# Keys of a sparse-attention layer projected transposed and rotated by a partition shuffle

## Chip, core and metric

The kernel runs on one core of a Trainium2 chip. The metric is the device time of one execution in microseconds (us). A profiled execution gives the rows quoted below; its engines are PE (TensorE matmuls), PEld (TensorE weight loads), DVE (VectorE), ACT (ScalarE), POOL (GpSimd) and SP (SyncE, which issues the DMAs).

## What is computed

Two layers over 256 tokens of width 1024. Each normalises its input, projects it once, and gives one part of the projection to a recurrent mixer (HGRN2) and one to a sparse attention with 8 query heads and 2 key/value groups of 128 dimensions. The part that matters here:

```python
q = partial_rope(q, pos)
ks = partial_rope(ks, pos)
kw = partial_rope(kw, pos)
k_cmp = compress(kc, *cmp_k)
v_cmp = compress(vc, *cmp_v).astype(jnp.float32)
k_cmp = partial_rope(k_cmp, cmp_end).astype(jnp.float32)
```

`ks`, `kw` are the keys of the selected-block and the window branch, `k_cmp` the 15 compressed keys. `partial_rope` rotates the first 32 of 128 dimensions only: with x1 the first 16 and x2 the next 16, it gives x1·cos − x2·sin and x2·cos + x1·sin; the other 96 pass through.

## The kernel before

**Precision and weights.** Every float32 matmul operand is split in a high and a low part, and a product takes three matmuls (high·high, high·low, low·high). Weights stream through a ring of units: a DMA lands in `raw`, ACT copies it to `whi` (L202) and DVE subtracts to `wlo` (L203). Eight converted units and five raw ones are held; a unit's place comes free with its last matmul. `Hhi` and `Hlo` are the transposed, normalised input with its dimensions on the partitions.

**The order of the work** is written out by hand. One layer runs: query projection (`a_pair`), forget gates, compressed keys and values (`kcvc`), `kv_w` (window keys and values), `compress` 0, `kv_s` (selected keys and values), `compress` 1, and then the attention, spread between the projections that follow. Later steps are handed to `later`, which emits them once a count of matmul time has passed (`tick`); `flush` emits them at once. Each engine then executes its own instructions in the order emitted.

**Keys, values and compress before.** `kv_s` multiplies with the tokens of one tile (`a`, 128 tokens) on the output partitions and 512 columns (256 of keys, 256 of values); `kv_w` does 256 key columns and 280 value and gate columns apart (L368 to L370, `mm_a`). So keys come out with tokens on the partitions: `rope` (L384) rotates them, ACT copying 96 dimensions (L386) and DVE doing four small operations (L390 to L393). Eight units of matmul time later `turn_k` turns them with PE transposes (L552), and `split_k` (L539) splits the result into `kTh` (copied by ACT, L540) and `kTl` (subtracted by DVE, L541), with the dimensions on the partitions as the scores (L608 to L610) want them. The compressed keys take the same way: `second` projects them (L519), `rope` rotates them, `third` transposes them (L531). Values go through `vals` (L558): a copy `vhi` on ACT (L560), then a subtraction `vlo` on DVE (L561). In `kv_w` a sigmoid on ACT (L587) reads the gate columns of the same bank after that.

**PSUM banks.** There are three banks of tag `mm`, two of `s`, two of `t`, one of `o`. In `kv_w` the values of tile 0 take one `s` bank, those of tile 1 the other, and `compress` 0 (L490 to L493, output `ps_s`) the first again: its first matmul waits for the last reader of tile 0's values, which is the sigmoid of L587. Two engines that read one bank do so one after the other.

Of the kernel before, what the change touches and what calls it, by code (L numbers as in the profile page):

```python
# [10 lines left out]
F32 = mybir.dt.float32  # L11
# [8 lines left out]
T = 256  # L20
# [11 lines left out]
C_KC, C_KS, C_KW, C_NG, C_NZ = 5120, 5632, 6144, 6656, 6680  # L32
SCALE = HD ** -0.5
LEVELS = (1, 2, 4, 8, 16, 32)
CTW = 544
SAFE = 1e-35
UW = 1072
RING = 8
# [3 lines left out]
CP = (2.0, 3.0)  # L42
L1 = (3.0, 3.0)
L2 = (5.0, 5.0)
L3 = 3.0
LQ = 4.0
LK = 8.0
LH = 10.0
PW = 7.0
PS = 48.0  # L50
# [2 lines left out]
def shape_tables():  # L53
    def rope(pos, scale):
        inv = np.float32(500000.0) ** (np.float32(-2.0) * np.arange(RH, dtype=np.float32) / np.float32(32))
        ang = pos.astype(np.float32)[:, None] * inv.astype(np.float32)[None, :]
        c = np.cos(ang.astype(np.float64)).astype(np.float32)
        s = np.sin(ang.astype(np.float64)).astype(np.float32)
        return np.concatenate([c, c, -s, s], axis=1) * np.float32(scale)

    t = np.arange(T)
    j = np.arange(128)
    parts = [np.eye(128, dtype=np.float32)]
    for scale in (SCALE, 1.0):
        r = rope(t, scale)
        parts.append(r[:128])
        parts.append(r[128:])
    e = 16 * np.arange(NCMP) + 31
    rc = np.zeros((128, 64), np.float32)
    rc[:NCMP] = rope(e, 1.0)  # L70
    parts.append(rc)
    for a in range(NT):
        cm = np.where(e[None, :] <= (a * 128 + j)[:, None], 0.0, NEG)
        parts.append(np.concatenate([cm, np.full((128, 1), NEG / 10)], axis=1).astype(np.float32))
    sel = np.zeros((128, 2, 30), np.float32)
    for part in range(2):
        for a in range(2):
            for g in range(G):
                for n in range(NCMP):
                    sel[34 * part + 16 * g + n + a, a, 15 * g + n] = 1.0  # L80
            sel[34 * part + 32 + a, a, :] = 1.0
    parts.append(sel.reshape(128, 60))
    f = np.concatenate(parts, axis=1).astype(np.float32)
# [9 lines left out]
    return f, f2, m  # L93


def build(ctx, tc, A, out):
# [150 lines left out]
    rope_k = [ct[:, 256 + 64 * a:320 + 64 * a] for a in range(NT)]  # L247
    rope_c = ct[:, 384:448]
    cmask = [ct[:, 448 + 16 * a:464 + 16 * a] for a in range(NT)]
    sel = ct[:, 480:540].rearrange("p (a n) -> p a n", a=2)  # L250
    cm3 = cp.tile([128, 384], BF, name="cm3")

    posh = cp.tile([128, 128], F32R, name="posh")
# [119 lines left out]
    def mm_b(ps, un, u, c):  # L373
        for i in range(4):
# [112 lines left out]
    def compress(l, i, ring, KC):  # L487
# [25 lines left out]

        def second():
            y2 = tb()
            n = 96 if i else NCMP
            for g in range(G):
                lhs = act3[:, g, :] if i else act[:, g * 15:(g + 1) * 15]
                P.matmul(out=y2[0:n, g * 128:(g + 1) * 128], lhsT=lhs, rhs=w2[:, i, :], start=True, stop=True)  # L519
            y2v = y2[0:n, 0:256].rearrange("p (g d) -> p g d", g=2)  # L520
            if i:
                S.copy(out=vcs[0:96], in_=y2v)
                V.tensor_tensor(out=vcs[32:64], in0=y2v[32:64], in1=vcs[32:64].bitcast(F32), op=OP.subtract)
                return
            kst = sp.tile([128, 2, 128], F32, name="kst", tag="st", bufs=2)
            rope(kst[0:NCMP], y2v, rope_c, 2, 1.0, NCMP)

            def third():
                tp = tb()
                for g in range(G):  # L530
                    P.transpose(out=tp[:, g * 128:g * 128 + NCMP], in_=kst[0:NCMP, g, :],  # L531
                                identity=ident[0:NCMP, 0:NCMP])
                split_k(256, NCMP, tp.rearrange("p (g n) -> p g n", g=4)[:, 0:2, 0:NCMP])

            later(L3, third, "c0")

        later(L1[i], sums, "c%d" % i)

    def split_k(o, n, src):  # L539
        S.copy(out=kTh[:, :, o:o + n], in_=src)  # L540
        V.tensor_tensor(out=kTl[:, :, o:o + n], in0=src, in1=kTh[:, :, o:o + n].bitcast(F32), op=OP.subtract)  # L541

    KOFF = ((128, 0), (272, 400))

    def keys(a, br, ps):
        kst = sp.tile([128, 2, 128], F32, name="kst", tag="st", bufs=2)
        rope(kst, ps.rearrange("p (g d) -> p g d", g=2), rope_k[a], 2, 1.0)

        def turn_k():
            tp = tb()  # L550
            for g in range(G):
                P.transpose(out=tp[:, g * 128:(g + 1) * 128], in_=kst[:, g, :], identity=ident)  # L552
            o = KOFF[br][a]
            split_k(o, 128, tp[:, 0:256].rearrange("p (g t) -> p g t", g=2))

        later(LK, turn_k, "k")

    def vals(a, br, ps):  # L558
        hi, lo = vhi[:, a, br, :], vlo[:, a, br, :]
        S.copy(out=hi, in_=ps)  # L560
        V.tensor_tensor(out=lo, in0=ps, in1=hi.bitcast(F32), op=OP.subtract)  # L561

    def kv_s(ring):
        un = ring.take(4)
        for a in range(NT):
            ps = mmb()
            for u in range(4):
                mm_a(ps, un[u], u, a, 0, 512)
                if a:
                    ring.done(1)  # L570
            keys(a, 0, ps[:, 0:256])
            vals(a, 0, ps[:, 256:512])

    def kv_w(ring):
        un = ring.take(4)
        for a in range(NT):
            ps = mmb()
            for u in range(4):
                mm_a(ps[:, 0:256], un[u], u, a, 0, 256)
            keys(a, 1, ps[:, 0:256])  # L580
            ps = sb_()
            for u in range(4):
                mm_a(ps[:, 0:280], un[u], u, a, 256, 280)
                if a:
                    ring.done(1)
            vals(a, 1, ps[:, 0:256])
            S.activation(out=gt[:, a].rearrange("p h b -> p (h b)"), in_=ps[:, 256:280], func=AF.Sigmoid)  # L587

    def attend(a, g):
# [8 lines left out]
        def scores(i):  # L598
# [16 lines left out]
                mk = [cm3[:, 128:256]] * 2  # L615
                cm = ps[:, 128:144]
            else:
                flush("k")
                qk(ps[:, 0:272], 0, 272)
                p2 = sb_()  # L620
                qk(p2[:, 0:256], 272, 528)
# [553 lines left out]
```

## Time and profile before

| | |
|---|---|
| runs of the kernel before | 559.06 us median (558.58 to 559.13, 3 runs) |
| profiled execution, its own time | 558.97 us |
| its span, first to last instruction | 557.2 us |
| busy: PE / PEld / DVE / ACT | 543.8 / 487.6 / 398.8 / 333.0 us |
| `kv_w` to `compress` 1, first layer | about 72 to 105 us from the span's start |
| the same, second layer | about 340 to 374 us |

The span leaves about 1.8 us around it. A group of the profile is a source line with an engine and an operation; a view by time shows start, duration and, in brackets, the idle time before an instruction and what ended it. Matmul durations overlap, since the next one starts while the last still drains: the distance from one start to the next is what a matmul costs.

### The profile page before, as it was taken

The page shows a single profiled execution, that of the slowest core. Times are in us where ns is not written, and L with a number is a line of the kernel's source. Part 1 is how long each engine was busy: PE and PEld are TensorE (multiplying, and loading weights), DVE is VectorE, ACT ScalarE, POOL GpSimd, SP SyncE. Part 2 cuts the span into 40 slices and gives each one's busy share as a digit, 9 for nine tenths or more (in the row PEclk, how much of TensorE's full clock was granted, in tenths as well). Part 3 has the DMA queues.
Part 4 walks back from the last instruction along what each step waited for, and adds up shares of the span by engine and source line. Part 5 has one row for each costly group of instructions (what it writes and reads, how often), then busy time and mean ns, then how long its engine had stood idle before and what let it go on. Part 6 is the DMA issues. An engine that isn't in the chain of part 4 may idle for free.

```text
span 557.2 us, 9821 instructions
## 1 busy us (share of the span) xinstructions
PE 543.8 (98%) x3675; PEld 487.6 (88%) x3675; DVE 398.8 (72%) x883; ACT 333.0 (60%) x632; POOL 9.6 (2%) x18
## 2 busy tenths in 40 slices
PE   7999999999999999999999999989999999999994
PEld 4889998899888989988888999979988888898884
DVE  4887997889777277563687599888987654866422
ACT  6576537865567685562557763677646768746311
POOL 4000000000000001001000000000000000000000
PEclk9999999999999999999999999999999999999998
DMA  8698548965146158566385755697433622956111
GB/s 302 195 314 257 146 127 266 304 193 152 39 117 190 35 166 291 185 191 188 115 262 162 228 154 152 196 302 256 125 101 84 174 85 63 303 172 200 59 38 44
DMA packets 72197, 96.56 MB, mean 173 GB/s; under 512 B 3383, under 2 KB 49357, under 8 KB 72142
## 3 DMA queue, kind: packets, MB, share of 16 engines
q1 hardware_dynamic: 71854, 95.33, 55.2%
q8 instruction: 31, 0.51, 0.4%
q10 hardware_dynamic: 288, 0.52, 0.2%
q14 instruction: 24, 0.20, 0.1%
HBM read 93.75 MB, written 2.10 MB: 172 GB/s over the span
## 4 chain that ended last, share of the span: by engine, by line
PE 88%; DMA 4%; ACT 3%; DVE 2%; issue 1%; SPq 0%; ACTq 0%; DVEq 0%
PE ps_mm L378 10%; PE ps_mm L380 10%; PE ps_mm L379 10%; PE ps_mm L368 9%; PE ps_mm L369 9%; PE ps_mm L370 9%; PE ps_mm L1005 4%; PE ps_mm L1007 4%; PE ps_mm L1006 4%; DMA raw<-in_w_in 2%; ACT whi L202 2%; PE ps_t L668 2%; DMA raw<-in_cmp_w_v 2%; PE ps_s L608 1%; DVE wlo L203 1%
## 5 line engine op out<-in xcount | busy, mean ns | idle before, releaser
L203 DVE TENSOR_TENSOR wlo<-raw,whi 128x1024 fp32r<-128x1024 f32 (+1 forms) x168 | 203.0, 1223 | 60.7 <-ACT whi L202 56.3
L202 ACT CAST whi<-raw 128x1024 fp32r<-128x1024 f32 (+1 forms) x168 | 174.9, 1052 | 87.9 <-PE ps_mm L379 24.5
L378 PE MATMUL ps_mm<-Hhi,whi 128*128 128x256 f32 x448 | 127.5, 285 | 0.0
L380 PE MATMUL ps_mm<-Hhi,wlo 128*128 128x256 f32 x448 | 125.7, 281 | 0.0
L379 PE MATMUL ps_mm<-Hlo,whi 128*128 128x256 f32 x448 | 125.7, 281 | 0.0
L368 PE MATMUL ps_mm<-whi,Hhi 128*128 128x512 f32 (+1 forms) x256 | 102.0, 399 | 0.7 <-ACT Hhi L355 0.7
L370 PE MATMUL ps_mm<-whi,Hlo 128*128 128x512 f32 (+1 forms) x256 | 98.9, 386 | 0.0
L369 PE MATMUL ps_mm<-wlo,Hhi 128*128 128x512 f32 (+1 forms) x256 | 98.8, 386 | 0.0
L379 PEld LDWEIGHTS ps_mm<-Hlo,whi 128*128 128x128 f32 x448 | 84.5, 189 | 0.1
L378 PEld LDWEIGHTS ps_mm<-Hhi,whi 128*128 128x128 f32 x448 | 84.3, 188 | 0.1
L380 PEld LDWEIGHTS ps_mm<-Hhi,wlo 128*128 128x128 f32 x448 | 84.4, 188 | 0.0
L370 PEld LDWEIGHTS ps_mm<-whi,Hlo 128*128 128x128 f32 x256 | 48.7, 190 | 10.3 <-DVE Hlo L356 0.3
L368 PEld LDWEIGHTS ps_mm<-whi,Hhi 128*128 128x128 f32 x256 | 48.9, 191 | 8.5 <-ACT Hhi L355 1.1
L369 PEld LDWEIGHTS ps_mm<-wlo,Hhi 128*128 128x128 f32 x256 | 49.0, 191 | 7.5 <-DVE wlo L203 0.5
L630 ACT ACTIVATE sB<-ps_s,nm 128x256 f32<-128x256 f32 (+1 forms) x40 | 16.9, 428 | 12.2 <-DVE nm L627 11.5
L627 DVE CUSTOM_DVE_ANT_0 ps_s<-ps_s,cm 128x128 f32<-128x128 f32 (+1 forms) x64 | 22.4, 371 | 1.9 <-PE ps_s L610 0.7
L671 DVE TENSOR_TENSOR sB<-ps_t,sB 128x512 fp32r<-128x512 f32 x12 | 8.3, 688 | 20.1 <-ACT sB L670 20.1
L1005 PE MATMUL ps_mm<-whi,sN 128*128 128x512 f32 x48 | 19.0, 397 | 0.0
L1006 PE MATMUL ps_mm<-wlo,Hhi 128*128 128x512 f32 x48 | 18.9, 395 | 0.0
L1007 PE MATMUL ps_mm<-whi,Hlo 128*128 128x512 f32 x48 | 18.9, 395 | 0.0
L1006 PE MATMUL ps_mm<-wlo,sN 128*128 128x512 f32 x48 | 18.9, 394 | 0.0
L1007 PE MATMUL ps_mm<-whi,sN 128*128 128x512 f32 x48 | 18.9, 394 | 0.0
(299 smaller groups left out, 921.0 us busy)
## 6 DMA issues: line engine op xcount, KB each, us to landing
raw<-in_w_in SPq DMA_DIRECT2D x112, 512.0 KB, 4.5
raw<-in_w_out SPq DMA_DIRECT2D x32, 512.0 KB, 4.3
raw<-in_w_in SPq DMA_DIRECT2D x8, 536.0 KB, 4.1
raw<-in_cmp_w_k SPq DMA_DIRECT2D x16, 256.0 KB, 3.4
raw<-in_cmp_w_v SPq DMA_DIRECT2D x16, 256.0 KB, 3.2
sB<-in_x SPq DMA_DIRECT2D x3, 512.0 KB, 3.6
sB<-in_post_norm SPq DMA_DIRECT2D x2, 512.0 KB, 4.8
xs<-sB SPq DMA_DIRECT2D x4, 256.0 KB, 2.0
```

The source lines that it names most:

```text
L202: S.copy(out=hi, in_=raw)
L203: V.tensor_tensor(out=lo, in0=raw, in1=hi.bitcast(F32), op=OP.subtract)
L368: P.matmul(out=ps, lhsT=hh, rhs=wh, start=k == 0, stop=False)
L369: P.matmul(out=ps, lhsT=hh, rhs=wl, start=False, stop=False)
L370: P.matmul(out=ps, lhsT=hl, rhs=wh, start=False, stop=k == KT - 1)
L378: P.matmul(out=ps, lhsT=wh, rhs=hh, start=k == 0, stop=False)
L379: P.matmul(out=ps, lhsT=wh, rhs=hl, start=False, stop=False)
L380: P.matmul(out=ps, lhsT=wl, rhs=hh, start=False, stop=k == KT - 1)
L627: V.tensor_tensor_reduce(out=sb[b], in0=sb[b], in1=mk[b], scale=-1.0, scalar=3e38, op0=OP.add, op1=OP.min, accum_out=nm[:, i, b:b + 1])
L1005: P.matmul(out=ps, lhsT=hi, rhs=wh, start=first, stop=False)
L1006: P.matmul(out=ps, lhsT=hi, rhs=wl, start=False, stop=False)
L1007: P.matmul(out=ps, lhsT=lo, rhs=wh, start=False, stop=last)
```

## The change

Keys are projected with the weights as the stationary operand and all 256 tokens as the moving one (L551 to L553 of the changed kernel, in `keys`), one group after the other, into one bank: 48 matmuls of 256 columns for each branch. The dimensions are on the partitions at once, so `turn_k`, `third` and their transposes go. `rope_t` rotates in place: a shuffle of the 32 partitions swaps the halves into `sh`, and three DVE operations multiply with tables and add, on 32 partitions. `split_k` then reads the bank directly. `second` projects the compressed keys in one matmul with 30 columns. Values of both token tiles in `kv_s` share one bank and are split by one ACT and one DVE operation. The table `ct` shrinks from 544 to 352 columns of 128 partitions; a table `kt` of 32 partitions and 544 columns is loaded later, in `consts2`.

```diff
-CTW = 544
+CTW = 352
+KTW = 544
...
+        nc.sync.dma_start(out=kt, in_=A["kt"])
...
+    def rope_t(x, tab, n):
+
+        c, s = (t[:, None, :].to_broadcast([32, G, n]) for t in tab)
+        sh = sp.tile([128, 512], F32, name="sh", tag="st", bufs=2)[0:32, 0:G * n].rearrange("p (g n) -> p g n", g=G)
+        V.stream_shuffle(out=sh, in_=x[0:32], mask=SWAP)
+        V.tensor_tensor(out=sh, in0=sh, in1=s, op=OP.mult)
+        V.tensor_tensor(out=x[0:32], in0=x[0:32], in1=c, op=OP.mult)
+        V.tensor_tensor(out=x[0:32], in0=x[0:32], in1=sh, op=OP.add)
...
+            if not i:
+                P.matmul(out=y2[:, 0:G * NCMP], lhsT=w2[:, 0, :], rhs=act, start=True, stop=True)
+                y2v = y2[:, 0:G * NCMP].rearrange("p (g n) -> p g n", g=G)
+                rope_t(y2v, rope_c, NCMP)
+                split_k(kTh[:, :, 256:256 + NCMP], kTl[:, :, 256:256 + NCMP], y2v)
+                return
...
-    def keys(a, br, ps):
-        kst = sp.tile([128, 2, 128], F32, name="kst", tag="st", bufs=2)
-        rope(kst, ps.rearrange("p (g d) -> p g d", g=2), rope_k[a], 2, 1.0)
-
-        def turn_k():
-            tp = tb()
-            for g in range(G):
-                P.transpose(out=tp[:, g * 128:(g + 1) * 128], in_=kst[:, g, :], identity=ident)
-            o = KOFF[br][a]
-            split_k(o, 128, tp[:, 0:256].rearrange("p (g t) -> p g t", g=2))
-
-        later(LK, turn_k, "k")
...
+    def keys(un, br):
+        ps = mmb()
+        for g in range(G):
+            out = ps[:, g * T:(g + 1) * T]
+            for k in range(KT):
+                wh, wl = (t[:, k % 2, g * 128:(g + 1) * 128] for t in un[k // 2])
+                P.matmul(out=out, lhsT=wh, rhs=Hhi[:, :, k, :], start=k == 0, stop=False)
+                P.matmul(out=out, lhsT=wh, rhs=Hlo[:, :, k, :], start=False, stop=False)
+                P.matmul(out=out, lhsT=wl, rhs=Hhi[:, :, k, :], start=False, stop=k == KT - 1)
+                tick(3 * 256 / 2400.0)
+        rope_t(ps.rearrange("p (g t) -> p g t", g=G), rope_k, T)
+        if br:
+            split_k(kTh[:, :, 272:528], kTl[:, :, 272:528], ps.rearrange("p (g t) -> p g t", g=G))
...
     def kv_s(ring):
         un = ring.take(4)
+        keys(un, 0)
+        ps = mmb()
         for a in range(NT):
-            ps = mmb()
             for u in range(4):
-                mm_a(ps, un[u], u, a, 0, 512)
+                mm_a(ps[:, a * 256:(a + 1) * 256], un[u], u, a, 256, 256)
                 if a:
                     ring.done(1)
-            keys(a, 0, ps[:, 0:256])
-            vals(a, 0, ps[:, 256:512])
+        vals(vhi[:, :, 0, :], vlo[:, :, 0, :], ps.rearrange("p (a d) -> p a d", a=NT))
 
     def kv_w(ring):
         un = ring.take(4)
+        keys(un, 1)
         for a in range(NT):
-            ps = mmb()
-            for u in range(4):
-                mm_a(ps[:, 0:256], un[u], u, a, 0, 256)
-            keys(a, 1, ps[:, 0:256])
             ps = sb_()
             for u in range(4):
                 mm_a(ps[:, 0:280], un[u], u, a, 256, 280)
                 if a:
                     ring.done(1)
-            vals(a, 1, ps[:, 0:256])
+            vals(vhi[:, a, 1, :], vlo[:, a, 1, :], ps[:, 0:256])
             S.activation(out=gt[:, a].rearrange("p h b -> p (h b)"), in_=ps[:, 256:280], func=AF.Sigmoid)
```

Two places show how instructions move. DVE in `kv_w` of the first layer, from the last weight unit before the rotation (`wlo`), before:

```order
L203 TENSOR_TENSOR wlo<-raw,whi 128x1024
L390 TENSOR_TENSOR rt_951<-ps_mm,ct 128x64
L391 TENSOR_TENSOR kst<-ps_mm,ct 128x2x16
L392 TENSOR_TENSOR kst<-ps_mm,ct 128x2x16
L393 TENSOR_TENSOR kst<-kst,rt_951 128x2x32
L561 TENSOR_TENSOR vlo<-ps_s,vhi 128x256
```

and in the changed kernel:

```order
L201 TENSOR_TENSOR wlo<-raw,whi 128x1024
L389 STREAM_SHUFFLE sh<-ps_mm 32x512
L391 TENSOR_TENSOR ps_mm<-ps_mm,kt 32x512
L390 TENSOR_TENSOR sh<-sh,kt 32x512
L392 TENSOR_TENSOR ps_mm<-ps_mm,sh 32x512
L543 TENSOR_TENSOR kTl<-ps_mm,kTh 128x2x256
L564 TENSOR_TENSOR vlo<-ps_s,vhi 128x256
```

The low part of tile 0's values (`vlo`) stood behind four operations on one tile's keys; it now stands behind the rotation of both tiles' keys and their split.

ACT at the same place, from the last copy of compressed keys and values (`sN`), before:

```order
L477 CAST sN_917<-ps_mm 128x16x16 x2
L386 ACTIVATE kst<-ps_mm 128x2x96
L560 CAST vhi<-ps_s 128x256
L587 ACTIVATE gt<-ps_s 128x24
L386 ACTIVATE kst<-ps_mm 128x2x96
L202 CAST whi<-raw 128x1024 x3
```

and in the changed kernel:

```order
L487 CAST sN_919<-ps_mm 128x16x16 x2
L542 CAST kTh<-ps_mm 128x2x256
L563 CAST vhi<-ps_s 128x256
L200 CAST whi<-raw 128x1024
L587 ACTIVATE gt<-ps_s 128x24
L200 CAST whi<-raw 128x1024 x2
```

The split of the rotated window keys (`kTh`) has come ahead of the values' copy and the sigmoid (`gt`), and one weight copy has come between those two.

## Rows read from the trace of the kernel before

**Rows 1.** The page: chain that ended last, by engine, shares of the span.

```profile
PE 88%; DMA 4%; ACT 3%; DVE 2%; issue 1%; SPq 0%; ACTq 0%; DVEq 0%
```

**Rows 2.** Who PE waited for: us in total, times, longest.

```profile
PE ps_t L531 <- ACT whi L202: 1.4, 1, 1.4
...
PE ps_t L531 <- DVE kst L393: 0.6, 1, 0.6
```

**Rows 3.** PE by time, first `kv_s`: start us, us, engine, line, operation, shape.

```profile
89.61 0.40 PE L369 MATMUL ps_mm<-wlo,Hhi 128*128 128x512 f32 x1
89.84 0.40 PE L370 MATMUL ps_mm<-whi,Hlo 128*128 128x512 f32 x1
```

**Rows 4.** PE by time: a key transpose pair, the compressed keys' projection, their transposes.

```profile
104.63 0.28 PE L492 MATMUL ps_s<-whi,sN 128*68 128x256 f32 x1
104.75 0.28 PE L493 MATMUL ps_s<-wlo,sN 128*68 128x256 f32 x1
104.87 0.38 PE L552 MATMUL ps_t<-ct,kst 128*128 128x128 f32 x2
...
105.20 0.28 PE L493 MATMUL ps_s<-wlo,sN 128*68 128x256 f32 x1
...
98.22 0.40 PE L370 MATMUL ps_mm<-whi,Hlo 128*128 128x512 f32 x1
...
99.42 0.40 PE L369 MATMUL ps_mm<-wlo,Hhi 128*128 128x512 f32 x1
...
370.65 0.28 PE L493 MATMUL ps_s<-wlo,sN 128*68 128x256 f32 x1
372.33 0.27 PE L531 MATMUL ps_t<-ct,kst 15*128 15x15 f32 x2 [1.40 <-ACT whi L202]
...
372.70 0.28 PE L493 MATMUL ps_s<-wlo,sN 128*68 128x256 f32 x1
```

**Rows 5.** All engines by time around the sigmoid and `compress` 0, both layers.

```profile
81.89 0.23 DVE L390 TENSOR_TENSOR rt<-ps_mm,ct 128x64 f32<-128x64 f32 x1
...
83.24 2.95 ACT L202 CAST whi<-raw 128x1024 fp32r<-128x1024 f32 x3
...
84.04 0.38 PE L552 MATMUL ps_t<-ct,kst 128*128 128x128 f32 x2
...
350.04 0.22 DVE L390 TENSOR_TENSOR rt<-ps_mm,ct 128x64 f32<-128x64 f32 x1
...
350.36 1.22 DVE L203 TENSOR_TENSOR wlo<-raw,whi 128x1024 fp32r<-128x1024 f32 x1
...
351.63 0.42 DVE L561 TENSOR_TENSOR vlo<-ps_s,vhi 128x256 fp32r<-128x256 f32 x1
...
352.09 0.19 ACT L587 ACTIVATE gt<-ps_s 128x24 f32<-128x24 f32 x1 [2.80 <-DVE vlo L561]
...
352.33 0.34 PE L492 MATMUL ps_s<-whi,sN 128*68 128x256 f32 x1
```

**Rows 6.** DVE by time: two operations back to back, 512 elements on 128 partitions.

```profile
332.62 0.68 DVE L811 TENSOR_TENSOR sA<-sA,ce 128x512 f32<-128x512 f32 x1
333.23 0.69 DVE L814 TENSOR_TENSOR sA<-sA,kx 128x512 f32<-128x512 f32 x1
```

**Rows 7.** Groups by form on DVE and ACT: busy, mean ns of one, idle before.

```profile
L435 DVE TENSOR_TENSOR qlo<-ps_t,q 128x512 fp32r<-128x512 f32 x8 | 5.5, 688 | 0.0
...
L434 ACT CAST q<-ps_t 128x512 fp32r<-128x512 f32 x8 | 4.7, 584 | 0.4 <-PE ps_t L430 0.4
```

**Rows 8.** Stretches: length; busy PE, PEld, DVE, ACT, POOL; granted clock, DMA share, GB/s.

```profile
0.00:9.60 9.60, 5.72 (x12) 2.73 (x12) 2.41 (x7) 4.77 (x10) 5.93 (x15) 1.00 0.76 256
9.60:15.90 6.30, 6.26 (x14) 4.39 (x15) 5.81 (x9) 5.76 (x10) 0.00 (x0) 1.00 1.04 394
370.60:372.30 1.70, 0.33 (x3) 0.08 (x2) 1.67 (x6) 1.58 (x2) 0.00 (x0) 1.00 0.87 248
549.70:557.20 7.50, 0.00 (x0) 0.00 (x0) 2.04 (x5) 0.77 (x3) 0.00 (x0) 0.64 0.22 76
```

More of the change, by code (lines that the diff above doesn't have):

```diff
@@ L44 @@
 L2 = (5.0, 5.0)
-L3 = 3.0
 LQ = 4.0
-LK = 8.0
 LH = 10.0
@@ L63, in shape_tables @@
     parts = [np.eye(128, dtype=np.float32)]
[L64 to L67, printed above, removed]
+    r = rope(t, SCALE)
+    parts.append(r[:128])
+    parts.append(r[128:])
     e = 16 * np.arange(NCMP) + 31
-    rc = np.zeros((128, 64), np.float32)
-    rc[:NCMP] = rope(e, 1.0)
-    parts.append(rc)
     for a in range(NT):
@@ L92, in shape_tables @@
     m = np.ascontiguousarray(np.concatenate(ms, axis=1).astype(np.float32))
-    return f, f2, m
+    rows = [r[:, i:i + 32].T for r in (rope(t, 1.0), rope(e, 1.0)) for i in (0, 32)]
+    kt = np.concatenate(rows, axis=1).astype(np.float32)
+    kt = np.ascontiguousarray(np.pad(kt, ((0, 0), (0, KTW - kt.shape[1]))))
+    return f, f2, m, kt
 def build(ctx, tc, A, out):
@@ L246, in build @@
     rope_q = [ct[:, 128 + 64 * a:192 + 64 * a] for a in range(NT)]
[L247 to L250, printed above, removed]
+    cmask = [ct[:, 256 + 16 * a:272 + 16 * a] for a in range(NT)]
+    sel = ct[:, 288:348].rearrange("p (a n) -> p a n", a=2)
+    kt = cp.tile([32, KTW], F32, name="kt")
+    rope_k = (kt[:, 0:256], kt[:, 256:512])
+    rope_c = (kt[:, 512:512 + NCMP], kt[:, 512 + NCMP:512 + 2 * NCMP])
+    SWAP = [(i + 16) % 32 for i in range(32)]
     cm3 = cp.tile([128, 384], BF, name="cm3")
@@ L515, in second @@
             y2 = tb()
-            n = 96 if i else NCMP
-            for g in range(G):
[L518 to L524, printed above, removed]
@@ L525, in second @@
-            kst = sp.tile([128, 2, 128], F32, name="kst", tag="st", bufs=2)
-            rope(kst[0:NCMP], y2v, rope_c, 2, 1.0, NCMP)
-            def third():
-                tp = tb()
-                for g in range(G):
[L531 to L535, printed above, removed]
@@ L537, in compress @@
-        later(L1[i], sums, "c%d" % i)
[L539 to L543, printed above, removed]
-    def keys(a, br, ps):
-        kst = sp.tile([128, 2, 128], F32, name="kst", tag="st", bufs=2)
-        rope(kst, ps.rearrange("p (g d) -> p g d", g=2), rope_k[a], 2, 1.0)
-        def turn_k():
-            tp = tb()
-            for g in range(G):
-                P.transpose(out=tp[:, g * 128:(g + 1) * 128], in_=kst[:, g, :], identity=ident)
-            o = KOFF[br][a]
-            split_k(o, 128, tp[:, 0:256].rearrange("p (g t) -> p g t", g=2))
-        later(LK, turn_k, "k")
@@ L558, in vals @@
-    def vals(a, br, ps):
-        hi, lo = vhi[:, a, br, :], vlo[:, a, br, :]
+            if not i:
[4 more added lines that the diff above has]
+                return
+            for g in range(G):
+                P.matmul(out=y2[0:96, g * 128:(g + 1) * 128], lhsT=act3[:, g, :], rhs=w2[:, i, :], start=True,
+                         stop=True)
@@ new lines, in second, with split_k @@
+            y2v = y2[0:96, 0:256].rearrange("p (g d) -> p g d", g=2)
+            S.copy(out=vcs[0:96], in_=y2v)
+            V.tensor_tensor(out=vcs[32:64], in0=y2v[32:64], in1=vcs[32:64].bitcast(F32), op=OP.subtract)
+        later(L1[i], sums, "c%d" % i)
+    def split_k(hi, lo, src):
+        S.copy(out=hi, in_=src)
+        V.tensor_tensor(out=lo, in0=src, in1=hi.bitcast(F32), op=OP.subtract)
+    def keys(un, br):
[11 more added lines that the diff above has]
+            split_k(kTh[:, :, 272:528], kTl[:, :, 272:528], ps.rearrange("p (g t) -> p g t", g=G))
+        else:
+            hi, lo = (t[:, :, 0:256].rearrange("p g (a t) -> p g a t", a=NT)[:, :, ::-1, :] for t in (kTh, kTl))
+            split_k(hi, lo, ps.rearrange("p (g a t) -> p g a t", g=G, a=NT))
@@ L560, in vals @@
+    def vals(hi, lo, ps):
         S.copy(out=hi, in_=ps)
@@ L617, in scores @@
             else:
-                flush("k")
                 qk(ps[:, 0:272], 0, 272)
@@ L1166 @@
     arrays = {n: np.ascontiguousarray(inputs[n]) for n in _INS}
-    arrays["ct"], arrays["ct2"], arrays["lm"] = shape_tables()
+    arrays["ct"], arrays["ct2"], arrays["lm"], arrays["kt"] = shape_tables()
     A = {n: nc.dram_tensor("in_" + n, a.shape, mybir.dt.from_np(a.dtype), kind="ExternalInput").ap()
```

## The prediction

> **What bounds the kernel now.** I first read the chain that ended last by engine: PE holds 88% of the span [rows 1]. What shortens another engine's work is therefore worth nothing unless PE waits for it; what takes matmul time from PE is worth its full length. Next I asked whom PE waited for: after the first 10 us there are only two waits, both of `third`'s transposes (L531), 0.6 us in the first layer and 1.4 us in the second [rows 2]. PE's own price is the distance from start to start: 0.23 us for 512 columns [rows 3], 0.12 us for 256 [rows 4]. Matmuls of 512 cut into two of 256, as the new `keys` and `kv_s` do, cost nothing more: two starts of 0.12 us against one of 0.23 are the same within the reading's 0.01.
>
> The sum is made against the profiled execution's 558.97 us; the median of the runs is 559.06, so the profile stands 0.09 below it. I give totals against the median.
>
> **What PE saves.**
> - Key transposes. From the matmul before a pair, 104.75, to the second one after it, 105.20, are 0.45 us [rows 4]. Two plain matmuls start in that time and take 0.23; the pair costs the other 0.22 us. There are two branches, two tiles and two layers, hence 8 pairs: **1.75 us**.
> - `third`. In the second layer the same distance is 370.65 to 372.70 [rows 4]. Of these 2.05 us two plain matmuls take 0.23, and 1.82 is lost: 1.40 the wait, 0.42 the two transposes. The first layer loses 0.6 + 0.42 = 1.02. Sum **2.85 us**.
> - `second`, keys. From 98.22 to 99.42 is 1.20 us [rows 4]; two matmuls of 512 columns start in it (at 98.22, and one behind the float32 products L519), so the products take 1.20 − 2 × 0.23 = 0.73 us a layer. Two products of 128 columns become one of 30. The gain lies between 0 (a float32 product's time is mostly fixed) and 0.73; I take half for the two layers' 1.46: **0.7 us**.
> - Start. `ct` is 192 columns narrower, 128 × 192 × 4 bytes = 98 KB less ahead of the first weights; at 256 GB/s [rows 8] that is 0.38 us. It counts only if these bytes hold the first matmul: between 0 and 0.4, I take **0.2 us**. `kt` (70 KB) comes later, behind other constants on SP's queue; it is first wanted tens of us later and costs nothing.
>
> Together **5.5 us**; by the bounds of the last two 4.6 to 6.4.
>
> **What PE newly waits for.** DVE's operations on the keys were short (64 elements, 0.23 us [rows 5]) and now handle 512. Ordinarily that is free: scores need the keys only after the projections that follow. But `compress` 0 writes into the `s` bank that tile 0's values have left, and its first matmul waits for the sigmoid `gt` (L587), the last to read that bank. In the second layer before, `gt` runs 352.09 to 352.28 and the first matmul of `compress` 0 starts at 352.33 [rows 5]: already just held. In the changed kernel there stand ahead of `gt`, on DVE, the shuffle, two products, an addition, `kTl` and `vlo`; on ACT `kTh`, `vhi` and one weight copy. Priced in order:
> 1. DVE, four rotation operations. Back to back 512 elements start 0.61 apart and the last ends after 0.69 [rows 6]. Two steps, a whole product, then the addition, which needs the product: 1.22 + 0.69 + 0.68 = 2.59. They use 32 partitions, but one operation's time follows the elements on each partition, so I make no discount.
> 2. `kTh`, an ACT cast of 512 elements: 0.58 [rows 7].
> 3. Now two strands. DVE: `kTl` 0.61 (its kin takes 688 ns alone [rows 7]), `vlo` 0.42 [rows 5], two hand-overs of 0.04 (352.09 − 351.63 − 0.42 [rows 5]): 1.11. ACT: `vhi` at half of 0.58, say 0.3, then a weight copy at 2.95 / 3 = 0.98 [rows 5], whose data had landed before: 1.28. ACT ends later.
> 4. `gt` 0.19 [rows 5] and two more hand-overs, 0.08.
>
> Sum 2.59 + 0.58 + 1.28 + 0.19 + 0.08 = 4.7 us from DVE's reaching the rotation. In the first layer DVE reached it at 81.89, held by earlier work; `gt` would end at 86.6. PE gets to `compress` 0 at 84.04, where the transposes L552 stood [rows 5]: a wait of **2.5 us**. In the second layer DVE reached it at 350.04, but the weight subtraction of 1.22 us that followed there [rows 5] now comes ahead: the rotation starts at 351.26, `gt` ends at 355.95. PE arrives at 352.33 less the 0.22 of the removed pair, 352.1: a wait of **3.85 us**. Sum **6.4 us**.
>
> The trace shows no shuffle. Its nearest rows are a short PSUM operation at 0.23 us and the weight subtraction of 1.22 [rows 5]; a gain is excluded, since the operation is added. I take 0.61 because the operation handles 512 elements; the bounds shift each layer by −0.4 and +0.55, so the loss is 5.6 to 7.5. The Trainium skill (VectorE: DVE Perf Modes, "The perf-mode tier table (the rule you actually need)") gives the shuffle a single rate, about 2400 ns at the table's size; scaled from 2048 elements to ours that is an estimate of 0.6 us, and the sum stays as it is. No row here shows it.
>
> `kv_s` and the compressed keys wait for nothing new: while PE stands, ACT and DVE convert the next weights, so the units that are now wanted earlier are ready, and the bank of `kv_s`'s values is one of the three `mm` banks. Behind the stall nothing can give time back, since PE has no slack [rows 2].
>
> Net without more: −5.5 + 6.4 = +0.9, **560.0 us** (by the bounds 558.3 to 562.0).
>
> **The clock.** The granted clock held 1.00 through the wait of 1.40 us [rows 8]. At the end of the kernel PE's last matmul is over at 549.70 and the stretch of 7.50 us behind it shows 0.64 [rows 8]: at full clock for x of it and half for the rest, x + 0.5 × (1 − x) = 0.64 gives x = 0.28, a fall 2.1 us after the last matmul. Both new waits, 2.5 and 3.85 us, lie beyond that, the second far beyond. What a fall costs is shown only by the start: 14 matmuls, nearly all of 512 columns, take 6.30 us from 9.60 to 15.90 [rows 8], 0.45 each instead of 0.23, half pace (although the column reads 1.00 there), a loss of 6.30 − 14 × 0.23 = 3.1 us. A fall during a wait in mid-kernel costs between 0 and 3.1; I take 2, nearer the row than nothing, because some of that stretch may have been the cold start's own.
>
> **The rivals.**
> - *One fall (the forecast)*, in the longer wait: 560.0 + 2 = **562.0 us**. For it: 3.85 is well above 2.1. Against: the end of the kernel is a single instance. Chance 0.33.
> - *Both fall*: 560.0 + 4 = **564.0 us**, 0.23. For it: 2.5 is also above 2.1; against: barely. [...]
> - *No fall*: **560.0 us**, 0.26. For it: the clock held at 1.40 [rows 8].
> - *Faster: the rotation starts early*. The point that decides is when DVE reaches it: the keys' last matmul comes some 6 us (48 steps of 0.12) before `compress` 0. If DVE got there then, 4.7 us would fit, no wait would come, and the time would be 559.06 − 5.5 = **553.6 us**. Against: in both layers DVE reached the earlier rotation of tile 0 only 2.1 and 2.3 us before PE got to `compress` 0, and did not idle ahead of it [rows 5]; the extra 256 columns of keys now come first. Chance 0.10.
> - *Slower still*: PSUM operations on 32 partitions or late weights in `kv_s` add 1 us or more per layer to both falls: 566 and above, 0.08. That the change does not do what it says would leave 559.06; transposes are gone from the order of PE, so I give that nothing.
>
> **How the numbers follow.** The forecast is the likeliest case, 562.0. The range runs from the low bound of no fall, 558.2, to both falls at 3.1 each, 566.2: it leaves out the faster rival and part of the slower one, under 2 in 10. About 0.2% (1.1 us) is what a measurement here can tell from no change. *Faster*: the rival's 0.10 and 0.02 of no fall at its low bound, 0.12. *Within*: most of no fall, 0.18, up to 560.2. *Slower*: 0.33 + 0.23 + 0.08 and the rest of no fall, 0.06: 0.70.
>
> **What the changed profile would show.** Right: the waits for L531 gone; two waits of `compress` 0's first matmul for ACT's `gt`, near 2.5 and 3.9 us; the chain running there through the rotation (L389 to L392) and `kTh`; the shuffle near 0.7 us; key matmuls 0.12 apart; a granted clock below 1.00, or matmuls at double distance, behind the second wait only. Wrong: no wait at `compress` 0 (faster rival), matmul distances unchanged behind both waits (no fall), doubled behind both, or a new wait in front of `kv_s`.

## Result and the profile after

The changed kernel takes 565.12 us (median of 4 runs, 564.32 to 565.85) against 559.10 for the kernel before on the same chip; the ratio is 1.0102, interval 1.0086 to 1.0119. It is slower, by 6.0 us where 2.9 were forecast. The profiled execution took 565.85 us with a span of 564.0, against 558.97 and 557.2.

The chain that ended last, by engine, against [rows 1]:

```profile
PE 83%; DVE 11%; issue 2%; ACT 2%; DMA 1%; SPq 0%; DVEq 0%; ACTq 0%
```

PE still leads, but 11% now run over DVE. Whom PE waited for (us in total, times, longest), against [rows 2]:

```profile
PE ps_s L502 <- ACT gt L587: 6.0, 2, 3.6
PE ps_s L608 <- ACT sN L629: 3.0, 2, 1.5
PE ps_mm L1087 <- DMA sB<-in_pre_norm: 2.2, 1, 2.2
PE ps_t L352 <- DVE sA L345: 1.4, 1, 1.4
```

The waits of `third` are gone. The first line is the forecast wait of `compress` 0 (now L502 and L503). The second is one that the forecast did not have: the scores (L608) wait for ACT's softmax, once in each layer, at the fourth scores behind `compress` 1. The last two lie in the first 10 us, as before.

Where the time went is read from the moments at which PE reaches the same weight unit in both traces (by time, PE):

| PE reaches | before | after | after − before |
|---|---|---|---|
| `kv_w`, layer 1 | 72.18 | 71.05 | −1.13 |
| `compress` 0 | 84.17 | 85.44 | +1.27 |
| `kv_s` | 87.98 | 90.77 | +2.79 |
| `compress` 1 | 100.59 | 102.79 | +2.20 |
| the projection behind it | 105.55 | 106.49 | +0.94 |
| the unit behind the fourth scores | 121.18 | 123.47 | +2.29 |
| `kv_w`, layer 2 | 340.22 | 342.57 | +2.35 |
| `compress` 0 | 352.33 | 358.18 | +5.85 |
| `kv_s` | 356.09 | 363.53 | +7.44 |
| `compress` 1 | 368.69 | 375.58 | +6.89 |
| the projection behind it | 374.44 | 379.29 | +4.85 |
| the unit behind the fourth scores | 390.07 | 396.40 | +6.33 |
| the last weight unit | 531.99 | 538.41 | +6.42 |

Each layer shows the same four steps: a jump up to `compress` 0 (2.40 and 3.50), another one through it (1.52 and 1.59), a gain until the projection behind `compress` 1 (1.85 and 2.59), and a loss at the scores (1.35 and 1.48). Between the layers nothing moves.

The first jump, in the first layer (all engines by time, against [rows 5]):

```profile
79.64 1.22 DVE L201 TENSOR_TENSOR wlo<-raw,whi 128x1024 fp32r<-128x1024 f32 x1
...
80.78 0.72 DVE L389 STREAM_SHUFFLE sh<-ps_mm 32x512 f32<-32x512 f32 x1
...
81.42 0.68 DVE L391 TENSOR_TENSOR ps_mm<-ps_mm,kt 32x512 f32<-32x512 f32 x1
...
82.02 0.67 DVE L390 TENSOR_TENSOR sh<-sh,kt 32x512 f32<-32x512 f32 x1
...
82.72 0.69 DVE L392 TENSOR_TENSOR ps_mm<-ps_mm,sh 32x512 f32<-32x512 f32 x1
...
83.50 0.58 ACT L542 CAST kTh<-ps_mm 128x512 fp32r<-128x512 f32 x1 [4.42 <-DVE ps_mm L392]
83.98 0.38 ACT L563 CAST vhi<-ps_s 128x256 fp32r<-128x256 f32 x1
84.11 0.69 DVE L543 TENSOR_TENSOR kTl<-ps_mm,kTh 128x512 fp32r<-128x512 f32 x1 [0.71 <-ACT kTh L542]
84.24 1.06 ACT L200 CAST whi<-raw 128x1024 fp32r<-128x1024 f32 x1
84.72 0.42 DVE L564 TENSOR_TENSOR vlo<-ps_s,vhi 128x256 fp32r<-128x256 f32 x1
85.19 0.20 ACT L587 ACTIVATE gt<-ps_s 128x24 f32<-128x24 f32 x1
...
85.44 0.39 PE L502 MATMUL ps_s<-whi,sN 128*68 128x256 f32 x1 [2.38 <-ACT gt L587]
```

This is the forecast chain, link by link: 80.78 to 85.39 is 4.6 us (forecast 4.7), the shuffle 0.72 alone and 0.64 to the next start, the products and the addition at the prices of [rows 6]. Behind `kTh` the two strands end together, where the forecast had ACT's end later: `vlo` is over at 85.14, and `gt` follows at 85.19, 0.95 behind the start of the weight copy ahead of it.

The second jump is the clock. Stretches of PE behind the two waits and one of `kv_s` (length; busy PE, PEld, DVE, ACT, POOL; granted clock, DMA share, GB/s), against [rows 8]:

```profile
85.44:88.83 3.39, 3.39 (x17) 3.39 (x17) 3.39 (x4) 3.39 (x6) 0.00 (x0) 0.52 0.25 76
358.18:362.20 4.02, 4.02 (x21) 4.02 (x22) 4.02 (x5) 4.02 (x6) 0.00 (x0) 0.58 0.29 81
363.53:366.30 2.77, 2.77 (x26) 2.77 (x25) 1.85 (x2) 1.31 (x2) 0.00 (x0) 1.00 0.89 248
```

The granted clock falls to about half (1.2 of 2.4 GHz) behind both waits. The matmuls show it too (PE by time):

```profile
88.61 0.42 PE L503 MATMUL ps_s<-wlo,sN 128*68 128x256 f32 x1
88.83 0.36 PE L502 MATMUL ps_s<-whi,sN 128*68 128x256 f32 x1
89.03 0.28 PE L503 MATMUL ps_s<-wlo,sN 128*68 128x256 f32 x1
89.14 0.28 PE L502 MATMUL ps_s<-whi,sN 128*68 128x256 f32 x1
```

They start 0.20 to 0.22 apart up to 89.03 and 0.11 to 0.12 from there on. All of `compress` 0 takes 5.33 and 5.35 us instead of 3.81 and 3.76: each fall costs 1.5 to 1.6 us here.

### The profile page after: what moved, and what is told of

The parts are those of the page before. It is cut to its first block, busy times and chain, and to the rows that moved or that the text cites. A ratio compares the mean times of both kernels' runs of the same rounds, so it can differ in the third digit from the quotient of the medians.

```text
span 564.0 us, 9925 instructions
## 1 busy us (share of the span) xinstructions
PE 543.5 (96%) x3747; PEld 493.0 (87%) x3747; DVE 403.8 (72%) x867; ACT 330.7 (59%) x616; POOL 9.6 (2%) x18
## 4 chain that ended last, share of the span: by engine, by line
PE 83%; DVE 11%; issue 2%; ACT 2%; DMA 1%; SPq 0%; DVEq 0%; ACTq 0%
PE ps_mm L369 9%; PE ps_mm L370 9%; PE ps_mm L371 9%; PE ps_mm L379 7%; PE ps_mm L380 7%; PE ps_mm L381 6%; PE ps_mm L1005 4%; PE ps_mm L1004 4%; PE ps_mm L1006 4%; DVE wlo L201 4%; PE ps_t L667 2%; PE ps_s L502 2%; PE ps_s L503 2%; PE ps_s L608 1%; PE ps_s L940 1%
## 5 line engine op out<-in xcount | busy, mean ns | idle before, releaser
L369 PE MATMUL ps_mm<-whi,Hhi 128*128 128x512 f32 (+1 forms) x224 | 88.7, 397 | 0.0
L371 PE MATMUL ps_mm<-whi,Hlo 128*128 128x512 f32 (+1 forms) x224 | 85.9, 384 | 0.0
L370 PE MATMUL ps_mm<-wlo,Hhi 128*128 128x512 f32 (+1 forms) x224 | 85.9, 384 | 0.0
L371 PEld LDWEIGHTS ps_mm<-whi,Hlo 128*128 128x128 f32 x224 | 42.5, 190 | 8.8 <-DVE Hlo L357 0.3
L369 PEld LDWEIGHTS ps_mm<-whi,Hhi 128*128 128x128 f32 x224 | 42.7, 191 | 6.2 <-ACT Hhi L356 0.4
L370 PEld LDWEIGHTS ps_mm<-wlo,Hhi 128*128 128x128 f32 x224 | 42.7, 191 | 6.3 <-DVE wlo L201 0.5
L502 PE MATMUL ps_s<-whi,sN 128*68 128x256 f32 x64 | 18.1, 314 | 6.0 <-ACT gt L587 6.0
L1004 PE MATMUL ps_mm<-whi,sN 128*128 128x512 f32 x48 | 19.1, 397 | 0.0
```

What stands on the lines that cost most here:

```text
L369: P.matmul(out=ps, lhsT=hh, rhs=wh, start=k == 0, stop=False)
L370: P.matmul(out=ps, lhsT=hh, rhs=wl, start=False, stop=False)
L371: P.matmul(out=ps, lhsT=hl, rhs=wh, start=False, stop=k == KT - 1)
L502: P.matmul(out=yp[0:68, 0:256], lhsT=KC[:, r, :], rhs=wh, start=r == 0, stop=False)
L1004: P.matmul(out=ps, lhsT=hi, rhs=wh, start=first, stop=False)
```

## Experiments

All runs are timed against the kernel before on their chip (558.5 to 559.0 us). The start of an execution varies by itself: PE reaches `kv_w` between 70.4 and 73.3 us in these traces, and between 70.4 and 72.2 among those with the changed start alone. So each profile is given by a second number, **from `kv_w` of the first layer to the last weight unit**: 531.99 − 72.18 = 459.8 us in the kernel before, 467.4 in the changed one.

### A bank of its own for `compress` 0 (run e1)

```diff
-        yp = sb_()
+        yp = sb_() if i else mmb()
```

> The changed kernel with one edit: compress 0 writes into a bank of tag mm instead of the s bank that tile 0's values leave. Theory (the wait is the bank's, nothing else of compress 0 needs the keys): both waits of compress 0's first matmul, 2.38 and 3.60 us, go, and with them the stretches of matmuls 0.21 us apart behind them, about 3 us where both show. The two waits of the scores L608, 1.5 us each, stay if they come from kv_s giving its weight places back late: 565.85 - 6.0 - 3.0 = about 556.8. Rival A: those waits at L608 are an after-effect of the stall (work bunched behind it): they go too, about 553.8. Rival B: DVE's and ACT's longer key work only moves the wait, to kv_s or to the next user of the bank: 559 or more.

Measured: 564.91 us, ratio 1.0106 (1.0085 to 1.0128); `kv_w` to the last unit 465.4. PE's waits:

```profile
PE ps_s L608 <- ACT sN L629: 5.5, 4, 1.5
...
PE ps_mm L553 <- DVE wlo L201: 2.1, 5, 0.8
```

The bank theory holds for the wait itself: L502 is gone, and with it the slow matmuls. But the time hardly moves. The keys of `kv_s` now wait for weight units, and the scores wait four times instead of twice. Rival B was right: the stall had covered these waits. The rotation stands in DVE's and ACT's queues ahead of the four units that `kv_s` wants within 2.8 us, and without the stall PE comes too early for them. A listed wait is less than what it costs, too (PE by time):

```profile
89.55 0.28 PE L552 MATMUL ps_mm<-Hlo,whi 128*128 128x256 f32 x1
90.31 0.39 PE L553 MATMUL ps_mm<-Hhi,wlo 128*128 128x256 f32 x1 [0.49 <-DVE wlo L201]
90.54 0.28 PE L551 MATMUL ps_mm<-Hhi,whi 128*128 128x256 f32 x1
```

The start distance is 0.76 instead of 0.12, a loss of 0.64 for a wait listed with 0.49, and the next distance is 0.23: the list counts idle time from the modelled end of the last matmul. In all, `kv_s` takes 13.85 and 15.00 us here against 12.02 and 12.05 in the changed kernel (from its first matmul to the first of `compress` 1): 4.8 us lost behind 2.1 listed. With the 2.5 us more at the scores this uses up most of the 9.1 that the stall and the slow matmuls had cost.

### Weight places given back earlier (run e2)

In `kv_s` the changed kernel multiplies the keys of both groups first, all four units, so no unit's place comes free before the last quarter of the work.

```diff
-        ps = mmb()
-        for a in range(NT):
-            for u in range(4):
-                mm_a(ps[:, a * 256:(a + 1) * 256], un[u], u, a, 256, 256)
-                if a:
-                    ring.done(1)
+        pv = [mmb(), mmb()]
+        for u in range(4):
+            for a in range(NT):
+                mm_a(pv[a][:, 0:256], un[u], u, a, 256, 256)
+            ring.done(1)
```

> The changed kernel with one edit: in kv_s the values of both tiles are multiplied unit by unit (two banks, split apart), so that a weight unit's place comes free 7.0, 8.4, 9.8 and 11.2 us after kv_s begins, as in the kernel before, instead of 9.1, 9.8, 10.5 and 11.2. Theory: the late places hold up the DMAs and conversions of the next units, and ACT's softmax stands behind them; so the two waits of 1.5 us at L608 go and all else stays: about 565.85 - 3.0 = 562.8 for an execution with both slow stretches. Rival (after-effect of the stall): nothing moves, 565 to 566.

Measured: 563.36 us, ratio 1.0081 (1.0056 to 1.0107); `kv_w` to the last unit 465.1, 2.2 less. The waits at L608 are gone, L502 stays:

```profile
PE ps_s L502 <- ACT gt L587: 6.0, 2, 3.6
```

The waits are as expected. That the profile gains 2.2 us and not 3.0 comes from the clock: behind the second wait, again 3.60 us long, the matmuls are slow from the first one on, and `compress` 0 takes 6.16 us there instead of 5.35. A fall can thus cost 2.4 us as well. How late places reach the scores can be followed in the changed kernel's trace (ACT, DVE and PE by time; the rows of each engine apart):

```profile
111.35 1.05 ACT L200 CAST whi<-raw 128x1024 fp32r<-128x1024 f32 x1 [1.11 <-DMA raw<-in_w_in]
...
114.16 2.00 ACT L200 CAST whi<-raw 128x1024 fp32r<-128x1024 f32 x2
...
115.24 2.36 DVE L201 TENSOR_TENSOR wlo<-raw,whi 128x1024 fp32r<-128x1024 f32 x2 [0.97 <-ACT whi L200]
117.52 0.17 DVE L624 TENSOR_TENSOR pc<-ps_s,ct 128x16 f32<-128x16 f32 x1
...
122.13 0.37 ACT L629 ACTIVATE sN<-ps_s,nm 128x128 f32<-128x128 f32 x1 [0.62 <-DVE pc L624]
...
122.99 0.39 PE L608 MATMUL ps_s<-kTh,q 128*128 128x272 f32 x1 [1.50 <-ACT sN L629]
```

A place that comes free late lets ACT convert late, so a `raw` buffer comes free late and the next DMA starts late; ACT then waits for data three times (one is shown). The two units copied at 114.16 stand on DVE ahead of the first softmax operation (`pc`), and the softmax of the second scores, whose bank the fourth scores take, is late. In the kernel before ACT waits for data too (0.97 and 1.13 us, at 104.16 and 106.64), but the same two units are copied at 111.55 and 112.76, and `pc` starts at 115.23 instead of 117.52. That early places take the wait away is shown; the way between is a reading of these rows.

### Both together (run e3)

> Both edits, own bank for compress 0 and unit by unit values in kv_s. If the two losses are separate: 565.85 - 6.0 - 3.0 - 3.0 = about 553.8, with no wait of PE above 0.3 us behind the first 10 us. If one is the other's cause, this equals the better of the two runs alone.

Measured: 562.05 us, ratio 1.0064 (1.0043 to 1.0086); `kv_w` to the last unit 463.4. Not 553.8: the waits for weight units (2.1 us, 5 times) and three waits at L608 (3.0) are there; `kv_s` takes 13.80 and 15.21 us, 4.9 more than in the changed kernel. Late places are not the only way to L608. A likely other one, which no run tests apart: ACT also stands still for the rotation of `kv_s`, with weight copies queued behind (ACT by time):

```profile
99.98 0.59 ACT L542 CAST kTh<-ps_mm 128x512 fp32r<-128x512 f32 x1 [1.31 <-DVE ps_mm L392]
100.47 2.00 ACT L200 CAST whi<-raw 128x1024 fp32r<-128x1024 f32 x2
```

### Late places in the kernel before (run e4)

```diff
         for a in range(NT):
             ps = mmb()
             for u in range(4):
-                mm_a(ps, un[u], u, a, 0, 512)
+                mm_a(ps[:, 0:256], un[u], u, a, 0, 256)
+            keys(a, 0, ps[:, 0:256])
+        ps = mmb()
+        for a in range(NT):
+            for u in range(4):
+                mm_a(ps[:, a * 256:(a + 1) * 256], un[u], u, a, 256, 256)
                 if a:
                     ring.done(1)
-            keys(a, 0, ps[:, 0:256])
-            vals(a, 0, ps[:, 256:512])
+            vals(a, 0, ps[:, a * 256:(a + 1) * 256])
```

> The kernel before with one edit: kv_s multiplies the keys of both tiles first and then the values, so that its weight places come free at 9.1, 9.8, 10.5 and 11.2 us, as in the changed kernel; no rotation by shuffle, no stall at compress 0. Theory of the late places: waits of about 1.5 us appear at L608 in both layers, 559.1 + 3.0 = 562.1. Rival (after-effect of the stall): 559.1, no such waits.

Measured: 558.60 us, ratio 0.9993 (0.9976 to 1.0009). The theory of late places alone fails here: the scores (here L612) wait once, 0.3 us. The test is stricter than meant: in the trace the last matmul of the first unit in `kv_s` starts 11.45 us behind the first matmul of `kv_s` (98.94 − 87.49), in the changed kernel 9.55 (100.32 − 90.77). In the kernel before, late places cost next to nothing. With the other parts of the change but no rotation the scores wait 1.2 us (e6, below), with the rotation 3.0: it takes both. That the rotation uses up slack of ACT and DVE is the reading of this, not shown apart.

### One part of the change alone (run e5)

The kernel before with the compressed keys' new way only (`second` in one product, `rope_t` of 30 columns, no `third`).

```diff
+            if not i:
+                P.matmul(out=y2[:, 0:G * NCMP], lhsT=w2[:, 0, :], rhs=act, start=True, stop=True)
+                y2v = y2[:, 0:G * NCMP].rearrange("p (g n) -> p g n", g=G)
+                rope_t(y2v, rope_cT, NCMP)
+                split_k(256, NCMP, y2v)
+                return
```

> The kernel before with one part of the change alone: the compressed keys projected in one product with 30 columns and rotated by shuffle there (30 elements per operation); selected and window keys keep tokens on the partitions, rope and transposes. Theory (the change's gain at third and second is free of its losses, which all come from 512-element operations): the waits 0.6 and 1.4 us at L531 and the two layers' transposes go, 559.0 - 2.85 - 0.7 = about 555.5, no new wait. Rival: something else of the same place ends just behind (the next weight unit, the next scores), and the waits move: 557 to 559.

Measured: 558.72 us, ratio 0.9992 (0.9975 to 1.0009); `kv_w` to the last unit 458.9, only 0.9 less. A miss, and the rival's case: something else ended just behind. PE's waits, and ACT by time at the second one (`st` is ACT's copy of `compress` 1's output, L514 in this kernel):

```profile
PE ps_t L519 <- ACT st L514: 1.9, 2, 1.2
```
```profile
375.95 1.04 ACT L205 CAST whi<-raw 128x1024 fp32r<-128x1024 f32 x1 [0.99 <-DMA raw<-in_w_in]
376.91 0.37 ACT L561 CAST kTh<-ps_t 128x256 fp32r<-128x256 f32 x1
377.17 0.37 ACT L514 COPY st<-ps_s 68x256 f32<-68x256 f32 x1
```

The copy stands behind a weight copy that waits for its DMA. With `third`'s wait gone PE is there earlier, and waits again.

### The rotation left out, or half of it (runs e6 and e7)

The next two kernels leave out part of the computation: the first the whole rotation of the selected and window keys, the second two of its four DVE operations.

```diff
-        rope_t(ps.rearrange("p (g t) -> p g t", g=G), rope_k, T)
```

> The changed kernel without the rotation of the selected and window keys (its four DVE operations of 512 elements are left out, twice a layer; the split stays). Theory (the length of the rotation on DVE, behind which ACT's kTh waits in order, is the root of all three losses): chain to gt shorter by 2.6 us, so waits of compress 0 of 0 and about 1.0 us, no matmuls 0.21 us apart, waits at L608 at most 0.3 each as in the kernel before with late places: about 555. Rival (places given back late, by themselves): the waits at L608 stay 1.5 each, about 557.5.

```diff
...
+        if n == T:
+            V.tensor_tensor(out=x[0:32], in0=x[0:32], in1=c, op=OP.mult)
+            V.tensor_tensor(out=x[0:32], in0=x[0:32], in1=s, op=OP.mult)
+            return
         V.stream_shuffle(out=sh, in_=x[0:32], mask=SWAP)
...
```

> The changed kernel with two of the four 512-element DVE operations of the rotation left out (two products in place stay; the keys are not rotated rightly). The chain to gt is shorter by about 1.3 us: waits of compress 0 of about 1.1 and 2.3 us. If the fall of the clock goes by the length of the wait, the first shows no slow matmuls behind it, and the second may, as the 2.38 us wait of the changed kernel did. Time about 565.85 - 2.6 - 1.5 (one slow stretch less) - 1 (L608 shorter) = 560.7, between the changed kernel and the one without rotation. Rival (any wait of more than 1 us costs a slow stretch): both slow, 562.2.

Measured: 555.40 us (ratio 0.9939, 0.9921 to 0.9958) without the rotation and 560.48 us (1.0033, 1.0019 to 1.0047) with half of it. Both times are as expected, but not all the waits. With none, PE waits 0.2 us at L502 (1.0 was expected), 1.2 at the scores (0.3 each at most) and 0.4 for `st`; with half of it (`compress` 0 is L507 there):

```profile
PE ps_s L507 <- ACT gt L592: 3.5, 2, 2.4
PE ps_s L613 <- ACT sN L634: 2.6, 2, 1.4
```

The waits of `compress` 0 go with the rotation's time on DVE ahead of `gt`: 6.0 us with all of it, 3.5 with half, 0.2 with none. The scores' waits go less evenly: 3.0, 2.6, 1.2. Half the operations take away somewhat less than half of the loss. One part missed: the waits are 1.1 and 2.4, and in this execution (559.36, one of the fastest of its twelve) neither has slow matmuls behind it, where the sum had kept one slow stretch (PE by time, second layer):

```profile
353.14 0.34 PE L507 MATMUL ps_s<-whi,sN 128*68 128x256 f32 x1 [2.36 <-ACT gt L592]
353.31 0.28 PE L508 MATMUL ps_s<-wlo,sN 128*68 128x256 f32 x1
353.43 0.28 PE L507 MATMUL ps_s<-whi,sN 128*68 128x256 f32 x1
```

### The floor (run e8)

Own bank, early places and no rotation of the selected and window keys (left out).

> Own bank for compress 0, places given back as early as before, and no rotation of the selected and window keys (its four DVE operations left out): what the change would be worth if nothing waited. 559.0 - 1.75 - 2.85 - 0.7 - 0.2 to 1.1 at the start = 552.6 to 553.5, with no wait of PE over 0.3 us behind the first 10 us. If waits remain, the kTh and kTl splits of 512 elements are long enough by themselves to cost something.

Measured: 553.58 us, ratio 0.9905 (0.9887 to 0.9923); `kv_w` to the last unit 454.5, **5.3 less than before**. Behind the first 10 us no wait of PE is listed. This is what the change saves on PE.

### The rotation later, nothing left out (run e9)

```diff
+        def turn():
+            rope_t(ps.rearrange("p (g t) -> p g t", g=G), rope_k, T)
...
+        later(LK[br], turn, "k")
...
             flush("c0")
+            flush("k")
```

Both entries of `LK` are 12.0 us; `turn` holds the split too. The two branches are moved together; no run moves one alone.

> The changed kernel, nothing left out, with the rotation and the split of both branches' keys handed to `later` and emitted 12 us of matmul time behind their projection (behind gt and the weight units of kv_s), and at the latest before the first scores. Theory (what costs is the rotation's place in DVE's and ACT's queues, ahead of gt and of weight conversions, not its length): waits of compress 0 gone, no slow matmuls; the waits at L608 between 0.3 and 1.5 each, since places still come free late: 554.5 to 557. Rival (the length costs wherever it stands, DVE having no room): waits reappear at the scores or at weight units, 559 or more.

Measured: **554.92 us, ratio 0.9932 (0.9917 to 0.9947)**, faster than the kernel before and about 10 us faster than the changed one, with the same operations in another order; `kv_w` to the last unit 456.3. DVE by time, first layer:

```profile
82.37 2.36 DVE L202 TENSOR_TENSOR wlo<-raw,whi 128x1024 fp32r<-128x1024 f32 x2 [0.70 <-ACT whi L201]
84.64 0.42 DVE L568 TENSOR_TENSOR vlo<-ps_s,vhi 128x256 fp32r<-128x256 f32 x1
84.98 3.48 DVE L202 TENSOR_TENSOR wlo<-raw,whi 128x1024 fp32r<-128x1024 f32 x3
...
88.39 0.73 DVE L390 STREAM_SHUFFLE sh<-ps_mm 32x512 f32<-32x512 f32 x1
```

Five weight units now come ahead of the rotation. What PE still waits for:

```profile
PE ps_s L613 <- ACT sN L634: 1.0, 2, 0.6
...
PE ps_s L614 <- DVE kTl L544: 0.3, 1, 0.3
```

The rival (length costs wherever it stands) falls: without any rotation (e6) the time was 555.40, no better. It is the place in the queues that costs.

### Later, with early places (runs e10, e11 and e12)

The edit of the second experiment added to this one.

> The run before with the values of kv_s multiplied unit by unit besides, so that weight places come free as early as before. If late places and the queue place are the two roots, this comes within about 1 us of the floor run without rotation (553.6): 553.6 to 555. If DVE's work as such is too much, the waits at L608 stay: 556 or more.

Measured: 556.51 us, ratio 0.9962 (0.9948 to 0.9977), slower than without it. The waits at L608 are gone, and a new one has come:

```profile
PE ps_mm L370 <- DVE kTl L544: 1.2, 2, 1.0
```

The values' second bank is the third of tag `mm`, still held by the window keys that wait for their late rotation.

> As the run before, with the selected keys rotated 7 us behind their projection instead of 12, window keys 12 as there: the split of the selected keys then stands ahead of four more weight units on ACT. If the place ahead of weight units is what makes L608 wait, this is slower than the run before by up to 1 us a layer, 554 to 557; if not, the same.

```diff
-LK = (12.0, 12.0)
+LK = (7.0, 12.0)
```

With the selected keys' lag at 7 us: 556.61 us, ratio 0.9964 (0.9950 to 0.9978), the same time; the wait for `kTl` is 2.6 us there. It tells nothing about the place on ACT, since the bank decides first. The profiled execution is the slowest of its twelve (558.51), and its longer wait has a fall of the clock behind it: matmuls 0.21 apart, with 0.50 granted from 364.87 to 366.37 (PE by time):

```profile
363.87 0.39 PE L370 MATMUL ps_mm<-whi,Hhi 128*128 128x256 f32 x1 [1.98 <-DVE kTl L544]
...
364.67 0.41 PE L372 MATMUL ps_mm<-whi,Hlo 128*128 128x256 f32 x1
364.88 0.41 PE L370 MATMUL ps_mm<-whi,Hhi 128*128 128x256 f32 x1
```

```diff
-        pv = [mmb(), mmb()]
+        pv = [mmb(), sb_()]
```

> The kernel e10_late_free with one word changed: the second value bank of kv_s is one of tag s instead of mm. Theory: e10's waits before the values of kv_s (0.2 and 1.0 us for the key split kTl) came from the third mm bank, which the late window keys still held; they go, no wait at L608 takes their place (there are none in e10), and the time falls below e9_late_keys by its remaining waits of 1.3 us: 553.6 to 554.6. Rival (e10 lost to e9 by ACT's and DVE's order, not by the bank): 556 to 557 as before.

Measured: **553.42 us, ratio 0.9900 (0.9881 to 0.9919)**, the fastest, with nothing left out and as fast as the floor. Behind the first 11 us PE waits for one thing:

```profile
PE ps_t L515 <- ACT st L510: 0.4, 1, 0.4
```

The bank was e10's loss.

## Why the prediction was right, and where it missed

- **Direction and range.** Slower, with 0.70; 565.12 lies in 558.2 to 566.2, near its upper end. That is in part luck: the upper end stood for two falls of 3.1 us each, and the time came near it by two falls of about 1.5 and by waits at the scores that the sum did not have. Nearest in kind was the rival *Slower still*, both falls and late weights; but the late weights showed at the scores, not in `kv_s`.
- **What PE saves.** The transposes, `third` and `second` were summed to 5.3 us; the floor run shows 5.3 between `kv_w` and the last unit. The total is better than its terms: the one product of `second` costs 0.22 us a layer (from 100.32 to 100.78, less two starts of 0.12) where 0.73 stood, so its part was 1.0 and not 0.7, and the rest came to less. The start gained 1.13 us in the profile of after, where 0.2 was taken. That it comes from the smaller table is not shown: starts vary by more than that among equal kernels.
- **What of it could be had.** Alone, the compressed keys' part gave 0.9 (e5). In the changed kernel the stretch from `kv_s` to the projection behind `compress` 1 gains 1.85 and 2.59 us, and in the floor run, which has no stall, it is as short (15.76 and 15.77 us, against 15.72 and 15.76). So the stall is not what makes the gain real; why the copy `st` comes late in e5 and in time in these two, no run shows.
- **The wait at `compress` 0.** Forecast 2.5 and 3.85, measured 2.38 and 3.60, by the chain as written. That it is the bank's, run e1 shows; that the rotation makes it long, e6 and e7 show.
- **The clock.** Both falls came in the profiled execution: the rival *Both fall*, not the forecast of one. Each costs 1.5 to 1.6 us where I took 2. Two of the four executions are 1.4 us faster than the other two, about one fall; that these have one fall less is inferred, they have no trace (their mean granted clock is 0.993, against 0.990 and 0.992 in the slower two). The 2.1 us read at the end of the kernel, by which both waits were judged, decides nothing: a fall came behind 1.98 us in e11 and none behind 2.36 in e7.
- **The step that failed** is "`kv_s` and the compressed keys wait for nothing new". The units for `kv_s` were ready, as said, but only thanks to the stall (2.1 us of waits in e1). And I followed the units only up to their first use, not to when their places come free. With all keys first, the first place of `kv_s` comes free with 9.1 of its 11.2 us of matmul time gone instead of 7.0; DMAs, conversions and the softmax behind them slip, and the scores wait 1.5 us in each layer. Run e2 shows the places' part in this; e4, e6 and e9 show that it takes the rotation's place ahead of other work as well. That the median misses the forecast by just these 3.0 us (565.1 − 562.0 = 3.1) is a coincidence. The profiled execution misses it by 3.9: 3.0 at the scores and 1.1 by the second fall, less 0.9 gained at the start and 0.4 at `compress` 0; the remaining 1.1 or so lies behind the last unit (0.4) and in what waits cost beyond their listed length.
- **The faster rival**, 553.6, named the right price and the wrong condition. The rotation need not come early; it may come late, since nothing needs the keys before the scores. Run e12 stands at 553.4.
- **What a page says of the clock.** The Trainium skill (TensorE: Matmul & The Clock Gate, "HAM oscillation — how this bites in real kernels") shows a kernel in which every wait for data of about 3 to 5 us between bursts of matmuls puts the array back to half clock. The wait of 3.60 us agrees, with 0.58 granted behind it. The waits of 2.38 us here (0.52) and 1.98 in e11 (0.50) are shorter than the page's and had a fall too; the wait of 2.36 us in e7, behind which matmuls start 0.12 apart, had none.

## What to carry to other kernels

When an operation gets longer on an engine that is not the bound, look at what stands behind it in its queue and which shared buffer the last of these releases; then hand the long work to a place where nothing behind it is due. Count, for every reordering, not only when an operand is first wanted but when its buffer comes free. A stall that is removed uncovers what was ready only because of it, so try a remedy together with the next wait in line.

## Not expected of the hardware

- The length of PE's wait alone did not decide whether the clock fell: behind 2.38 us the matmuls were slow from the start, behind 2.36 us they never were, and behind 3.60 us the first four started at the old pace (358.18 to 358.58) before they slowed to 0.21 apart. Behind the same 3.60 us in e2 they were slow from the start, and in e11 1.98 us was enough. In e2 the mean granted clock also differs between executions, from 0.986 to 0.996, and the fastest one (561.11) has the highest: the same kernel seems not to fall each time, but only one execution of it has a trace.
- The shuffle of 512 elements on 32 partitions took 0.72 us, as much as a product of the same size (0.68), and with 30 elements 0.18.
